# Four down-projection columns opened together at an FFN's end, and end columns that alternate between two pairs of PSUM banks

## The chip, the cores and the metric

The kernel runs on one core of a Trainium2 chip. The metric is the device time of one execution in microseconds (us), lower is better. The engines named below are TensorE (PE, matrix products; its weight loads are listed apart as PEld), VectorE (DVE), ScalarE (ACT), GpSimd (POOL) and SyncE (SP, which issues the transfers). SBUF is the core's working memory; PSUM is the accumulator memory that TensorE writes, eight banks of 128 partitions by 512 floats.

## The reference

A backbone of four layers (D = 1024) over 256 context tokens and 256 latent tokens. Each layer has a token mixer (0: windowed attention, 1: latent attention, 2: a gated linear recurrence, RG-LRU, 3: windowed attention again), and behind it a gated feed-forward network (FFN). Each of these eight stages ends in a projection back to 1024 columns whose gated result is added to the residual stream, and the next stage begins with an RMS norm of that stream.

```python
for layer in range(DEPTH):                      # DEPTH = 4
    kind, idx = layer % N_MIXERS, layer // N_MIXERS
    with_ctx_out = layer < DEPTH - 1
    ...
    h_lat = modulate(rmsnorm(x, norm1[layer]), sh1, sc1)
    h_ctx = modulate(rmsnorm(ctx, norm1[layer]), csh1, csc1)
    ...                                         # the mixer: y_lat, y_ctx (its last step is "... @ w_o")
    x = x + g1 * y_lat
    x = x + g2 * conv_ffn(modulate(rmsnorm(x, norm2[layer]), sh2, sc2), ...)
    if with_ctx_out:
        ctx = ctx + cg1 * y_ctx
        ctx = ctx + cg2 * conv_ffn(modulate(rmsnorm(ctx, norm2[layer]), csh2, csc2), ...)
return x

def conv_ffn(h, w_up, conv_w, conv_b, w_down):  # D_FF = 2816
    gate, val = jnp.split(h @ w_up, 2, axis=-1)
    gate = depthwise_conv(gate, conv_w, conv_b, FFN_CONV // 2)
    return (jax.nn.silu(gate) * val) @ w_down
```

The recurrent mixer projects h to a gate and an x branch (`lru_w_in`), convolves the x branch over four tokens, makes two sigmoid gates from it in each direction, scans, and projects the gated sum of both scans (`lru_w_out`).

## The kernel before

**Layout.** The residual stream is kept transposed, eight tiles `X[0..7]` of 128 columns by 512 tokens (0 to 255 context, 256 to 511 latent; layer 3 carries latents alone behind its mixer). A projection of all tokens is a product per 128 output columns, 512 wide.

**Products in three parts.** Each operand is kept as a high part (`hi`, rounded by ScalarE) and the rest (`lo`). `mm3` makes three TensorE products per pair of tiles: hi by hi (L227), the other side's lo (L228) and the weight's lo (L229). One output column of an FFN's last group with its four gated tiles is so 12 products.

**Weights.** SyncE loads a unit of 1024 columns (`raw`), ScalarE rounds it (`whi`, L214), GpSimd subtracts (`wlo`, L218). There are three buffers of `whi` and `wlo`: the unit after next can't be rounded before the products on the oldest one have run. A unit of the FFN's down projection (`fdn`) holds two output columns.

**PSUM.** Four pools with two banks each: `mm`, `fl`, `mo`, `tp`. A bank is free again when VectorE has added its column to X, at L452: `X = X + gate * column` ("x<-mo" in the profile, mo being the bank read).

**An FFN** goes through 22 gated tiles of 128 in groups, four in each but the first. ScalarE and VectorE make a gated tile (`fl`, L1117) and split it into `g_hi` (L261) and `g_lo` (L262). The products of a group with the down projection are made while the next group's up projections run; for the last group `out_tail` makes them.

**`out_tail`** ends every stage. It takes the eight output columns in units of `per` columns. In the layers that carry context the last three units' columns are made for the context half alone (256 wide) at first, and their weights are held; what is ahead of those is 512 wide. Then the next stage's norm is woven in: squares of the context half of X (ScalarE, L413) and their sum (VectorE, L415), two held columns for the latents (`lat(2)`), the sum over partitions (TensorE, L423), an inverse root of three Newton steps of VectorE on 128x2 numbers (L278, L268, L269, then L271 to L273 three times: `rs_v`, `rs_i`, `rs_y`, `rs_t`), its broadcast (TensorE, L427), the other held columns (`lat(99)`), and the normalised context (`hn`, L437). Attention stages end on `fl` banks (both ones), the FFNs and the recurrent layer on `mo` banks.

```python
for step, n in ((branch, 0), (branch, 1), (gates, 0), (branch, 2), (gates, 1), ...
lead = [(unit(("lix", m)), bank()) for m, bank in enumerate((fl_ps, fl_ps, mm_ps))]
```

**The recurrent layer** runs an order written by hand: `branch(n)` is the projection (`lix`, banks `fl`) and convolution (`xc`, L1001 and L1006) of two of eight column blocks, `gates(n)` the sigmoid gates (products of `x_hl` in banks `mm`, read at L1025) and the scans, `gate(n)` the GELU gate (`gg`, L1064). Its first three column blocks are made together ahead of it (`lead`). VectorE reads a block's bank four times (L1001, and L1006 for three taps) before it is free.

The order within each engine is set when the kernel is built: a scheduler puts the written order into one stream for each engine, and a free buffer of a pool is a condition of it.

Of the kernel before, what the change touches and what calls it, by code (L numbers as in the profile page):

```python
# [19 lines left out]
T = 512  # L20
NCTX = 256
DEPTH = 4
KT = D // 128
# [88 lines left out]
def hybrid_kernel(ctx: ExitStack, tc: tile.TileContext, xT, cc, ccT, W, modwa, modwb, modw, colv, rowv, tabs, band, out, depth=DEPTH, dbg=None):  # L112
# [43 lines left out]
    def mo_ps():  # L156
        return ps_mo.tile([128, T], F32, tag="mo", name="mo")

    def tp_ps():
        return ps_tp.tile([128, T], F32, tag="tp", name="tp")  # L160
# [3 lines left out]
    def dn_ps():  # L164
        turn[0] += 1
        return mo_ps() if turn[0] % 2 else tp_ps()

    X = [const.tile([128, T], F32, name=f"x{j}") for j in range(KT)]
    colt = const.tile([128, NCOLS], F32, name="colt")
# [274 lines left out]
                    nc.vector.scalar_tensor_tensor(lj, u, b, f32(hj), op0=ALU.add, op1=ALU.subtract)  # L444
            return op.ins

    def proj_cols(l, part, m, wt, src, sl, bank):
        ps = bank()
        mm3(ps[:, sl], [(wh, wl, sh[:, sl], sw[:, sl]) for (wh, wl), (sh, sw) in zip(wt, src)])
        for s, half in (CTX, LAT):  # L450
            if half.start >= sl.start and half.stop <= sl.stop:
                nc.vector.scalar_tensor_tensor(X[m][:, half], ps[:, half], modc[l][:, s, part + m:part + m + 1], X[m][:, half],  # L452
                                               op0=ALU.mult, op1=ALU.add)

    def out_tail(l, part, keys, per, src, t0, nxt, bank):
        n = len(src)

        def cols(z, wt):
            wh, wl = wt
            for m in range(z * per, (z + 1) * per):  # L460
                o = (m - z * per) * n
                yield m, [(wh[:, (o + k) * 128:(o + k + 1) * 128], wl[:, (o + k) * 128:(o + k + 1) * 128]) for k in range(n)]

        split_at = len(keys) if t0 else len(keys) - 3
        held = []
        for z, key in enumerate(keys):
            wt = unit(key)
            for m, w in cols(z, wt):
                proj_cols(l, part, m, w, src, slice(t0, T) if z < split_at else CTX[1], bank)
                if z >= split_at:  # L470
                    held.append((m, w))
        if held:
            todo = iter(held)

            def lat(k):
                for _ in range(k):
                    c = next(todo, None)
                    if c:
                        proj_cols(l, part, *c, src, LAT[1], bank)

            if isinstance(nxt, End):
                lat(99)
            else:
                nxt.tiles()
                sums = nxt.squares(1)
                lat(2)
                rb = nxt.rsq(sums)
                lat(99)
                nxt.apply(1, rb, range(KT))
                lat(99)  # L490
        nxt.half(0)
# [34 lines left out]
    def swa(l, i, q0, nm, nxt, first=None):  # L526
# [199 lines left out]
        for z, c in enumerate(cores[1]):  # L726
            core(*c)
            steps(mods, M1[z % len(M1)])
            for m in range(z * 8 // n, (z + 1) * 8 // n):
                half_proj(l, ("swo", i), m, units, tiles(*o[0]), q0 * 128)  # L730
        out_tail(l, 16, [("swo", i, 1, q) for q in range(4)], 2, tiles(*o[1]), q0 * 128, nxt, fl_ps)

    def mla(l, nm, nxt):
        hi, lo = nm.hi, nm.lo
# [194 lines left out]
        for hg in range(4):  # L929
            if hg < 3:  # L930
                group(hg + 1)
            for h in range(4):
# [9 lines left out]
                if hg == 3:  # L942
                    for m in (2 * h, 2 * h + 1):
                        half_proj(l, ("mwo",), m, units, tiles(*o[0]), 0)
        out_tail(l, 16, [("mwo", 1, q) for q in range(4)], 2, tiles(*o[1]), 0, nxt, fl_ps)

    def lru(l, nm, nxt):
        hi, lo = nm.hi, nm.lo
# [34 lines left out]
            in_part(wt, ps, slice(0, T))  # L983
            return ps

        lead = [(unit(("lix", m)), bank()) for m, bank in enumerate((fl_ps, fl_ps, mm_ps))]
        for _, sl in (CTX, LAT):
            for wt, ps in lead:
                in_part(wt, ps, sl)
# [77 lines left out]

        for step, n in ((branch, 0), (branch, 1), (gates, 0), (branch, 2), (gates, 1), (branch, 3), (gates, 2), (gate, 0), (gates, 3), (gate, 1), (merge, 0), (merge, 1), (gate, 2), (merge, 2), (gate, 3), (merge, 3)):
            step(n)
        out_tail(l, 16, [("lwo", m) for m in range(KT)], 1, tiles(rh[0], rl[0]) + tiles(rh[1], rl[1]), 0, nxt, mo_ps)  # L1070

    def ffn(l, t0, nm, nxt):
        hi, lo = nm.hi, nm.lo
# [72 lines left out]
                            next(mods, None)  # L1146
            pend = (a, b - a, gh, gl)
        a, n, gh, gl = pend
        out_tail(l, 40, [("fdn", l, a, q) for q in range(n)], KT // n, tiles(gh, gl, n), t0, nxt, mo_ps)

    def dump(n):
        if dbg is not None:
# [182 lines left out]
```

## Time and profile before

| | us |
|---|---|
| device time, median of three runs (2243.03 to 2250.57) | 2244.1 |
| profiled execution, its own time | 2239.54 |
| profiled execution, span of the trace | 2237.8 |
| TensorE busy in it | 2120.5 (95%) |
| VectorE busy | 1572.0 (70%) |
| ScalarE busy | 1033.3 (46%) |
| GpSimd busy | 1046.0 (47%) |

1.74 us of the profiled execution lie around its span. TensorE's records overlap by their pipelined ends, so that the busy share says where products run back to back, not how well; its idle time is what is to be read. In a row of the timeline the bracket gives the idle time of the engine ahead of that instruction and what ended it.

### The profile page before, as it was taken

The numbers are of one execution on the slowest core, as the hardware profiler recorded it, in microseconds if no ns is written. First come the engines' busy times: TensorE is split into PE (matmuls) and PEld (weight loads), VectorE is DVE, ScalarE is ACT, GpSimd is POOL, SyncE is SP. The second block draws the span as 40 slices with busy tenths as digits, with TensorE's granted clock in tenths as the row PEclk, the third lists the DMA queues.
The fourth block names the chain that finished last, engine by engine and source line by source line (L and its number), as shares of the span: only waits on it lengthen the run. The fifth ranks groups of instructions, "written<-read, shape, count | busy, mean of one in ns | idle before, by whom it ended". The sixth has DMA issues, their size and how long they took to land.

```text
span 2237.8 us, 32872 instructions
## 1 busy us (share of the span) xinstructions
PE 2120.5 (95%) x12084; PEld 1762.9 (79%) x12084; DVE 1572.0 (70%) x3342; ACT 1033.3 (46%) x1850; POOL 1046.0 (47%) x760
## 2 busy tenths in 40 slices
PE   6989999999999999999999998899999999898999
PEld 5666788888878666888888786688888887678999
DVE  4677779777776887687879689847864456785333
ACT  4467653332346775532323366634332234675544
POOL 3231155444544113444554456664544444526887
PEclk9999999999999999999999999999999999999999
DMA  8534136554532001155556422234655552313665
GB/s 300 195 123 133 39 131 193 170 173 164 174 101 68 21 29 57 60 194 175 175 179 189 140 67 81 78 93 136 194 185 167 164 168 74 104 38 107 187 181 158
DMA packets 83888, 300.14 MB, mean 134 GB/s; under 512 B 11152, under 2 KB 12816, under 8 KB 81296
## 3 DMA queue, kind: packets, MB, share of 16 engines
q1 hardware_dynamic: 83728, 298.05, 41.4%
q8 instruction: 95, 1.56, 0.3%
q14 instruction: 65, 0.53, 0.1%
HBM read 296.97 MB, written 1.05 MB: 133 GB/s over the span
## 4 chain that ended last, share of the span: by engine, by line
PE 76%; DVE 16%; ACT 4%; DMA 2%; issue 1%; POOL 1%; SPq 0%; ACTq 0%; DVEq 0%
PE fl L228 9%; PE fl L229 8%; PE fl L227 8%; PE mm L227 7%; PE mm L229 7%; PE mm L228 7%; PE mo L228 4%; PE mo L227 4%; PE mo L229 4%; PE tp L227 3%; PE tp L229 2%; PE tp L228 2%; PE mo L700 2%; PE mm L887 2%; PE tp L694 2%
## 5 line engine op out<-in xcount | busy, mean ns | idle before, releaser
L218 POOL TENSOR_TENSOR wlo<-raw,whi 128x256 fp32r<-128x256 f32 (+3 forms) x709 | 1011.4, 1448 | 1121.6 <-ACT whi L214 1086.0
L214 ACT ACTIVATE whi<-raw 128x1024 fp32r<-128x1024 f32 (+3 forms) x367 | 382.6, 1043 | 478.0 <-PE tp L228 187.8
L376 DVE SCALAR_TENSOR_TENSOR junk<-mw,cbc 128x1024 bf16<-128x1024 f32 x256 | 457.6, 1788 | 24.3 <-DMA mw<-in_modw_dram 14.7
L227 PE MATMUL fl<-h_hi,whi 128*128 128x512 f32 (+1 forms) x832 | 296.8, 358 | 3.3 <-DVE lam L961 1.7
L228 PE MATMUL fl<-h_lo,whi 128*128 128x512 f32 (+1 forms) x832 | 297.3, 358 | 0.2 <-POOL h_lo L442 0.2
L229 PE MATMUL fl<-h_hi,wlo 128*128 128x512 f32 (+1 forms) x832 | 297.2, 358 | 0.1
L228 PE MATMUL mm<-h_lo,whi 128*128 128x512 f32 (+1 forms) x768 | 269.8, 352 | 2.3 <-DVE h_lo L444 1.5
L227 PE MATMUL mm<-h_hi,whi 128*128 128x512 f32 (+1 forms) x768 | 270.6, 352 | 1.3 <-ACT h_hi L438 1.1
L229 PE MATMUL mm<-h_hi,wlo 128*128 128x512 f32 (+1 forms) x768 | 269.3, 351 | 0.0
L1112 DVE SCALAR_TENSOR_TENSOR conv<-mm,colt,conv 128x510 f32<-128x510 f32 (+1 forms) x88 | 59.8, 679 | 191.7 <-ACT conv L1110 191.7
L1116 ACT ACTIVATE conv<-conv 128x512 f32<-128x512 f32 (+1 forms) x88 | 51.0, 580 | 288.9 <-DVE conv L1114 288.9
L227 PEld LDWEIGHTS fl<-h_hi,whi 128*128 128x128 f32 x832 | 157.7, 190 | 26.2 <-DVE xc L1006 1.9
L228 PEld LDWEIGHTS fl<-h_lo,whi 128*128 128x128 f32 x832 | 158.2, 190 | 23.0 <-POOL h_lo L442 0.6
L229 PEld LDWEIGHTS fl<-h_hi,wlo 128*128 128x128 f32 x832 | 158.1, 190 | 22.9 <-POOL wlo L218 0.5
L227 PE MATMUL mo<-g_hi,whi 128*128 128x256 f32 (+1 forms) x488 | 164.8, 338 | 9.4 <-DVE x L452 6.3
L228 PE MATMUL mo<-g_lo,whi 128*128 128x256 f32 (+1 forms) x488 | 164.0, 336 | 0.4 <-DVE g_lo L262 0.4
L228 PEld LDWEIGHTS mm<-h_lo,whi 128*128 128x128 f32 x768 | 146.4, 191 | 22.8 <-DVE h_lo L444 2.3
L227 PEld LDWEIGHTS mm<-h_hi,whi 128*128 128x128 f32 x768 | 147.0, 191 | 21.0 <-ACT h_hi L438 1.9
L229 PE MATMUL mo<-g_hi,wlo 128*128 128x256 f32 (+1 forms) x488 | 163.5, 335 | 0.0
L229 PEld LDWEIGHTS mm<-h_hi,wlo 128*128 128x128 f32 x768 | 146.3, 191 | 18.6
L452 DVE SCALAR_TENSOR_TENSOR x<-mo,modc,x 128x256 f32<-128x256 f32 x212 | 95.4, 477 | 85.9 <-PE mo L229 85.6
L227 PEld LDWEIGHTS mo<-g_hi,whi 128*128 128x128 f32 x488 | 92.4, 190 | 21.9 <-DVE x L452 6.7
(313 smaller groups left out, 4376.0 us busy)
## 6 DMA issues: line engine op xcount, KB each, us to landing
raw<-in_W_dram SPq DMA_DIRECT2D x352, 512.0 KB, 3.6
mw<-in_modw_dram SPq DMA_DIRECT2D x144, 512.0 KB, 4.2
mw<-in_modwa_dram SPq DMA_DIRECT2D x8, 1024.0 KB, 16.2
mw<-in_modwb_dram SPq DMA_DIRECT2D x16, 512.0 KB, 4.7
mw<-in_modwb_dram SPq DMA_DIRECT2D x8, 1024.0 KB, 9.2
cbc<-in_cc_dram SPq DMA_DIRECT2D x3, 1024.0 KB, 5.8
raw<-in_W_dram SPq DMA_DIRECT2D x8, 384.0 KB, 3.0
x<-in_xT_dram SPq DMA_DIRECT2D x8, 256.0 KB, 3.7
```

Of the source, the lines that this page charges most:

```text
L214: nc.scalar.activation(hi, raw, AF.Copy)
L218: nc.gpsimd.tensor_tensor(lo[:, cs], raw[:, cs], f32(hi[:, cs]), op=ALU.subtract)
L227: nc.tensor.matmul(ps, ah, bh, start=start and i == 0, stop=False, **kw)
L228: nc.tensor.matmul(ps, ah, bl, start=False, stop=False, **kw)
L229: op = nc.tensor.matmul(ps, al, bh, start=False, stop=stop and i == n - 1, **kw)
L376: nc.vector.scalar_tensor_tensor(junk, raw, 1.0, cbc[:, s], op0=ALU.mult, op1=ALU.mult, accum_out=modc[l][:, s, m:m + 1])
L452: nc.vector.scalar_tensor_tensor(X[m][:, half], ps[:, half], modc[l][:, s, part + m:part + m + 1], X[m][:, half], op0=ALU.mult, op1=ALU.add)
L694: nc.tensor.transpose(pp[:, c:c + 128], P[z][:, (2 * kp + kk) * 128:(2 * kp + kk + 1) * 128], ident)
L700: nc.tensor.matmul(po[r], v[0][:, kb, p * 128 + 64 * z:p * 128 + 64 * z + 64], pt[:, kp, (kk * 2 + z) * 128:(kk * 2 + z + 1) * 128], start ...
L887: nc.tensor.matmul(ps[:, c], d["q"][:96, 2 * hp + z, bc], d["k"][:96, 2 * hp + z, :nk], start=True, stop=True)
L1112: op = nc.vector.scalar_tensor_tensor(y3[:, :, 1:], g3[:, :, :255], cw[:, l, 0, f:f + 1], y3[:, :, 1:], op0=ALU.mult, op1=ALU.add)
L1116: nc.scalar.activation(y[:, t0:], y[:, t0:], AF.Silu)
```

## The change

Four edits:

1. `tail_ps`, a new source of banks, alternates between `mo` and `fl`, four banks. The ends of the attention stages and of the recurrent layer take their columns from it.
2. An FFN's end takes columns 0 to 3 (two units of weights) in four banks at once (`opened`: mo, tp, mo, tp). All products with the first three gated tiles come first for these four columns, then the products with the last gated tile for each, then the additions to X. The other columns take `dn_ps` (mo and tp in turn), the held latent halves `tail_ps`.
3. `proj_cols` is split: its additions are `add_cols` now, which stands alone behind the opened columns.
4. The recurrent layer's three leading column blocks stand in banks mm, mm, fl, where they stood in fl, fl, mm.

```diff
+    def tail_ps():
+        turn[0] += 1
+        return mo_ps() if turn[0] % 2 else fl_ps()
...
-    def proj_cols(l, part, m, wt, src, sl, bank):
-        ps = bank()
-        mm3(ps[:, sl], [(wh, wl, sh[:, sl], sw[:, sl]) for (wh, wl), (sh, sw) in zip(wt, src)])
+    def add_cols(l, part, m, ps, sl):
         for s, half in (CTX, LAT):
             if half.start >= sl.start and half.stop <= sl.stop:
                 nc.vector.scalar_tensor_tensor(X[m][:, half], ps[:, half], modc[l][:, s, part + m:part + m + 1], X[m][:, half],
                                                op0=ALU.mult, op1=ALU.add)
...
-    def out_tail(l, part, keys, per, src, t0, nxt, bank):
+    def proj_cols(l, part, m, wt, src, sl, bank):
+        ps = bank()
+        mm3(ps[:, sl], [(wh, wl, sh[:, sl], sw[:, sl]) for (wh, wl), (sh, sw) in zip(wt, src)])
+        add_cols(l, part, m, ps, sl)
+
+    def out_tail(l, part, keys, per, src, t0, nxt, bank, last=None, opened=()):
         n = len(src)
...
-        for z, key in enumerate(keys):
-            wt = unit(key)
+
+        def begin(z):
+            wt = unit(keys[z])
+            got = []
             for m, w in cols(z, wt):
-                proj_cols(l, part, m, w, src, slice(t0, T) if z < split_at else CTX[1], bank)
+                sl = slice(t0, T) if z < split_at else CTX[1]
+                got.append((m, w, sl))
                 if z >= split_at:
                     held.append((m, w))
+            return got
+
+        z0 = 0
+        if opened:
+            z0 = len(opened) // per
+            parts = []
+            for z in range(z0):
+                for m, w, sl in begin(z):
+                    parts.append((m, w, sl, opened[m]()))
+
+            def term(w, k, sl):
+                return [(*w[k], src[k][0][:, sl], src[k][1][:, sl])]
+
+            for m, w, sl, ps in parts:
+                for k in range(n - 1):
+                    mm3(ps[:, sl], term(w, k, sl), start=k == 0, stop=False)
+            for m, w, sl, ps in parts:
+                mm3(ps[:, sl], term(w, n - 1, sl), start=False)
+                add_cols(l, part, m, ps, sl)
+        for z in range(z0, len(keys)):
+            for m, w, sl in begin(z):
+                proj_cols(l, part, m, w, src, sl, bank)
+        bank = last or bank
...
-        out_tail(l, 16, [("swo", i, 1, q) for q in range(4)], 2, tiles(*o[1]), q0 * 128, nxt, fl_ps)
+        out_tail(l, 16, [("swo", i, 1, q) for q in range(4)], 2, tiles(*o[1]), q0 * 128, nxt, tail_ps)
...
-        out_tail(l, 16, [("mwo", 1, q) for q in range(4)], 2, tiles(*o[1]), 0, nxt, fl_ps)
+        out_tail(l, 16, [("mwo", 1, q) for q in range(4)], 2, tiles(*o[1]), 0, nxt, tail_ps)
...
-        lead = [(unit(("lix", m)), bank()) for m, bank in enumerate((fl_ps, fl_ps, mm_ps))]
+        lead = [(unit(("lix", m)), bank()) for m, bank in enumerate((mm_ps, mm_ps, fl_ps))]
...
-        out_tail(l, 16, [("lwo", m) for m in range(KT)], 1, tiles(rh[0], rl[0]) + tiles(rh[1], rl[1]), 0, nxt, mo_ps)
+        out_tail(l, 16, [("lwo", m) for m in range(KT)], 1, tiles(rh[0], rl[0]) + tiles(rh[1], rl[1]), 0, nxt, tail_ps)
...
-        out_tail(l, 40, [("fdn", l, a, q) for q in range(n)], KT // n, tiles(gh, gl, n), t0, nxt, mo_ps)
+        out_tail(l, 40, [("fdn", l, a, q) for q in range(n)], KT // n, tiles(gh, gl, n), t0, nxt, dn_ps, tail_ps,
+                 (mo_ps, tp_ps, mo_ps, tp_ps))
```

What stands where, in the streams as built (the changed kernel's lines stand further down: its L231, L232, L233 are L227 to L229 of before, L454 is L452, L419 is L415).

TensorE at the end of layer 0's FFN, before: column 0 (bank `mo_5840`) makes its third and fourth gated tile's products and column 1 (`mo_5855`) begins; `g_hi_5375` and `g_lo_5376` hold all four gated tiles of the group.

```order
L227 MATMUL mo_5840<-g_hi_5375,whi_5836 128x512
L228 MATMUL mo_5840<-g_lo_5376,whi_5836 128x512
L229 MATMUL mo_5840<-g_hi_5375,wlo_5837 128x512
L227 MATMUL mo_5840<-g_hi_5375,whi_5836 128x512
L228 MATMUL mo_5840<-g_lo_5376,whi_5836 128x512
L229 MATMUL mo_5840<-g_hi_5375,wlo_5837 128x512
L227 MATMUL mo_5855<-g_hi_5375,whi_5836 128x512
L228 MATMUL mo_5855<-g_lo_5376,whi_5836 128x512
```

The same place now, from the last first-part product of column 3 (`tp_5849`) on: then the last gated tile's products of columns 0 to 3.

```order
L231 MATMUL tp_5849<-g_hi_5375,whi_5844 128x256
L232 MATMUL tp_5849<-g_lo_5376,whi_5844 128x256
L233 MATMUL tp_5849<-g_hi_5375,wlo_5845 128x256
L231 MATMUL mo_5840<-g_hi_5375,whi_5836 128x512
L232 MATMUL mo_5840<-g_lo_5376,whi_5836 128x512
L233 MATMUL mo_5840<-g_hi_5375,wlo_5837 128x512
L231 MATMUL tp_5841<-g_hi_5375,whi_5836 128x512
L232 MATMUL tp_5841<-g_lo_5376,whi_5836 128x512
L233 MATMUL tp_5841<-g_hi_5375,wlo_5837 128x512
L231 MATMUL mo_5848<-g_hi_5375,whi_5844 128x256
L232 MATMUL mo_5848<-g_lo_5376,whi_5844 128x256
L233 MATMUL mo_5848<-g_hi_5375,wlo_5845 128x256
```

The last gated tile's products of column 0 moved behind the 36 products that columns 0 to 3 make with the other three tiles; the number of products is the same.

VectorE at the same place, before: the two halves of columns 0 and 1 are added to X, then a sum of squares (`acc`) stands ahead of column 2.

```order
L262 TENSOR_TENSOR g_lo_5376<-fl_5801,g_hi_5375 128x512
L452 SCALAR_TENSOR_TENSOR x0_94<-mo_5840,modc0_124,x0_94 128x256 x2
L452 SCALAR_TENSOR_TENSOR x1_95<-mo_5855,modc0_124,x1_95 128x256 x2
L415 TENSOR_TENSOR acc_5976<-acc_5976,sq_5978 128x256
L452 SCALAR_TENSOR_TENSOR x2_96<-mo_5876,modc0_124,x2_96 128x256
L415 TENSOR_TENSOR P_6145<-P_6145,P_6147 128x256
L415 TENSOR_TENSOR acc_5976<-acc_5976,sq_5981 128x256
```

VectorE there now.

```order
L266 TENSOR_TENSOR g_lo_5376<-fl_5801,g_hi_5375 128x512
L454 SCALAR_TENSOR_TENSOR x0_94<-mo_5840,modc0_124,x0_94 128x256 x2
L454 SCALAR_TENSOR_TENSOR x1_95<-tp_5841,modc0_124,x1_95 128x256 x2
L454 SCALAR_TENSOR_TENSOR x2_96<-mo_5848,modc0_124,x2_96 128x256
L454 SCALAR_TENSOR_TENSOR x3_97<-tp_5849,modc0_124,x3_97 128x256
L419 TENSOR_TENSOR acc_5976<-acc_5976,sq_5978 128x256
L454 SCALAR_TENSOR_TENSOR x4_98<-mo_5910,modc0_124,x4_98 128x256
```

The additions of columns 2 and 3 moved ahead of the first sum of squares, and four banks are read where two were.

TensorE in the recurrent layer, around the third pair's gates, before: four products of the first GELU gate (`mo_12989`) stand between the gates' products (`mm_12902` and `mm_12927`, from `x_hl`).

```order
L229 MATMUL mm_12902<-x_hl_12581,wlo_12867 128x512
L227 MATMUL mo_12989<-h_hi_11942,whi_12982 128x512
L228 MATMUL mo_12989<-h_lo_11944,whi_12982 128x512
L229 MATMUL mo_12989<-h_hi_11942,wlo_12983 128x512
L227 MATMUL mo_12989<-h_hi_11942,whi_12982 128x512
L227 MATMUL mm_12927<-x_hl_12581,whi_12918 128x512
L228 MATMUL mm_12927<-x_hl_12581,whi_12918 128x512
```

There now: the last gate's products (`mm_12954`) run to their end, and the GELU gate begins behind them.

```order
L231 MATMUL mm_12954<-x_hl_12581,whi_12918 128x512
L232 MATMUL mm_12954<-x_hl_12581,whi_12918 128x512
L233 MATMUL mm_12954<-x_hl_12581,wlo_12919 128x512
L231 MATMUL mo_12989<-h_hi_11942,whi_12982 128x512
L232 MATMUL mo_12989<-h_lo_11944,whi_12982 128x512
L233 MATMUL mo_12989<-h_hi_11942,wlo_12983 128x512
```

The first GELU gate's first four products moved from within the third pair's gates to behind them. GpSimd's and SyncE's streams are the same as before.

## Rows read from the trace of the kernel before

**Rows 1.** The page: busy times, and the chain that ended last, by engine.

```profile
PE 2120.5 (95%) x12084; PEld 1762.9 (79%) x12084; DVE 1572.0 (70%) x3342; ACT 1033.3 (46%) x1850; POOL 1046.0 (47%) x760
...
PE 76%; DVE 16%; ACT 4%; DMA 2%; issue 1%; POOL 1%; SPq 0%; ACTq 0%; DVEq 0%
```

**Rows 2.** TensorE's waits: waited for, us in total, times, longest.

```profile
PE tp L427 <- DVE rs_y L273: 13.5, 11, 3.4
...
PE mo L227 <- ACT gg L1064: 8.8, 1, 8.8
...
PE mo L227 <- DVE x L452: 6.3, 8, 1.2
...
PE mo L227 <- ACT g_hi L261: 3.0, 2, 1.5
...
PE fl L227 <- DVE x L452: 2.1, 3, 0.9
```

**Rows 3.** Timeline of TensorE, end of layer 0's FFN: start, duration, [idle before].

```profile
633.97 0.50 PE L227 MATMUL mo<-g_hi,whi 128*128 128x512 f32 x1 [1.49 <-ACT g_hi L261]
634.69 0.50 PE L228 MATMUL mo<-g_lo,whi 128*128 128x512 f32 x1 [0.22 <-DVE g_lo L262]
...
642.29 0.38 PE L227 MATMUL mo<-g_hi,whi 128*128 128x256 f32 x1 [1.25 <-DVE x L452]
...
655.37 0.39 PE L227 MATMUL mo<-g_hi,whi 128*128 128x256 f32 x1 [0.42 <-DVE x L452]
...
657.58 0.71 PE L427 MATMUL tp<-tabt,rs_y 128*128 128x128 f32 x4 [0.98 <-DVE rs_y L273]
```

**Rows 4.** Windows of TensorE, three FFN ends: length, busy (products), PEclk, DMA, GB/s.

```profile
630.27:640.89 10.62, 8.91 (x49) 1.00 0.42 133
642.29:651.03 8.74, 8.74 (x73) 1.00 0.12 36
1855.54:1863.93 8.39, 8.39 (x48) 1.00 0.31 110
1865.50:1874.23 8.73, 8.73 (x72) 1.00 0.21 60
...
2222.48:2234.30 11.82, 11.72 (x97) 1.00 0.27 94
```

**Rows 5.** Timeline of VectorE, end of layer 0's FFN.

```profile
639.43 2.41 DVE L415 TENSOR_TENSOR acc<-acc,sq 128x256 f32<-128x256 f32 x1 [0.34 <-ACT sq L413]
...
644.02 0.43 DVE L415 TENSOR_TENSOR acc<-acc,sq 128x256 f32<-128x256 f32 x1 [0.48 <-ACT sq L413]
...
652.01 0.16 DVE L278 TENSOR_SCALAR rs_v<-tp 128x2 f32<-128x2 f32 x1 [0.30 <-PE tp L423]
...
656.88 0.64 DVE L273 SCALAR_TENSOR_TENSOR rs_y<-rs_t,rs_y 128x2 f32<-128x2 f32 x1
```

**Rows 6.** Timeline of ScalarE, end of layer 0's FFN.

```profile
633.34 0.58 ACT L261 ACTIVATE g_hi<-fl 128x512 fp32r<-128x512 f32 x1
638.04 1.06 ACT L214 ACTIVATE whi<-raw 128x1024 fp32r<-128x1024 f32 x1 [1.25 <-PE mo L228]
```

**Rows 7.** Timeline of GpSimd, end of layer 0's FFN.

```profile
639.17 2.39 POOL L218 TENSOR_TENSOR wlo<-raw,whi 128x1024 fp32r<-128x1024 f32 x1 [3.28 <-ACT whi L214]
```

**Rows 8.** Timeline of TensorE, end of layer 0's attention.

```profile
282.96 0.39 PE L227 MATMUL fl<-o,whi 128*128 128x256 f32 x1 [0.88 <-DVE x L452]
```

**Rows 9.** Timeline of VectorE at the same place.

```profile
279.14 0.16 DVE L278 TENSOR_SCALAR rs_v<-tp 128x2 f32<-128x2 f32 x1 [0.30 <-PE tp L423]
...
284.28 0.15 DVE L273 SCALAR_TENSOR_TENSOR rs_y<-rs_t,rs_y 128x2 f32<-128x2 f32 x1
```

**Rows 10.** Timeline of TensorE in the recurrent layer.

```profile
1321.80 0.47 PE L227 MATMUL fl<-h_hi,whi 128*128 128x512 f32 x1 [1.73 <-DVE lam L961]
...
1383.58 0.80 PE L227 MATMUL mm<-x_hl,whi 128*128 128x512 f32 x1 [6.19 <-ACT ex L1025]
```

**Rows 11.** A window of VectorE in the recurrent layer: length, busy (instructions).

```profile
1316.00:1350.00 34.00, 30.89 (x43) 1.00 0.31 93
```

## What the change should do to the time: the prediction

> **What bounds the kernel now.** The page comes first: TensorE is busy 95% of the span, and the chain that ended last lies on it for 76%, on VectorE for 16% [rows 1]. The change adds and removes no product, so that it can only take TensorE's idle time, some 5%, or move it. Where that time lies is in TensorE's waits: 6.3 us for additions to X that free an mo bank, 3.0 us for the last gated tile, 2.1 us for fl banks, 13.5 us for the inverse root, 8.8 us once for a GELU [rows 2]. The change aims at the first three. What each is worth depends on what ends last behind it, which the timelines of the stage ends tell.
>
> At the end of layer 0's FFN TensorE stops at three places in the columns [rows 3]: 1.49 us in column 0 for `g_hi`, 0.22 us for `g_lo`, and 1.25 us ahead of column 4, whose mo bank VectorE hasn't read. The last is a chain of three engines. The fourth weight unit is rounded at 638.04, when the oldest buffer is released [rows 6]; GpSimd subtracts for 2.39 us from 639.17 [rows 7]; VectorE's sum of squares beside it takes 2.41 us where its like takes 0.43 us [rows 5], and the addition that TensorE waits for stands behind that sum. So the four columns take 10.62 us with 8.91 us of work, and the next 72 products, up to the sum over partitions (L423), start 1.40 us behind their end [rows 4].
>
> **The change part by part, FFN ends.** The FFN of layer 2 shows the four columns without the gated tile's wait: 8.39 us for 24 products of 512 and 24 of 256 columns, and 72 products of 256 take 8.73 us [rows 4]. That is 0.121 us a short product and (8.39 - 24 x 0.121) / 24 = 0.228 us a long one.
>
> - *Last gated tile.* Now 18 long and 18 short products stand ahead of it: 18 x 0.228 + 18 x 0.121 = 6.3 us. The stage begins at 630.27, so it is asked for at 636.6. `g_hi` is there at 633.34 + 0.58 = 633.92 [rows 6], and the product with `g_lo` could start at 634.69 [rows 3]. The wait is gone with some 2 us to spare.
> - *Bank wait.* Column 4 takes the bank of column 0. Column 0's last product is over at about 636.6 + 3 x 0.228 + 0.2 = 637.5, and two additions, each about as long as the undisturbed sum of the same size, 0.43 us [rows 5], free the bank by 638.4; TensorE comes to it at 630.27 + 8.39 = 638.66. Columns 5, 6 and 7 have banks of which the additions stand ahead of the first sum of squares now. The sum will still be blocked beside GpSimd, but the addition behind it (column 4's) is needed for a bank only much later. The wait is gone.
> - *Weights.* Buffer 0 is now released by the last product of column 1, at 638.66 - 6 x 0.121 = 637.9, where rounding began at 638.04 before. So the fourth unit's low part is ready at about 637.9 + 1.06 + 2.39 = 641.4; column 6 needs it at 638.66 + 24 x 0.121 + 0.24 = 641.8. It just holds, by 0.4 us.
>
> The Trainium skill (SBUF — State Buffer, Who interferes with whom) says that a VectorE instruction with two inputs in SBUF is blocked by a GpSimd instruction that reads SBUF, and one with a single SBUF input isn't. The 2.41 us sum agrees. By that rule the four additions that now stand ahead of the sum, with one input in PSUM, run through GpSimd's subtraction.
>
> The sum over partitions then starts at 630.27 + 8.39 + 8.73 = 647.4 where it started at 651.03: 3.6 us. Behind it VectorE goes from 652.01 to 657.52 through the inverse root without a pause [rows 5]. The 0.42 us ahead of a held column at 655.37 may go through the other banks, but the broadcast waits for the root all the same, and its 0.98 us [rows 3] becomes so much longer. So nothing is won behind the sum: **-3.6 us**.
>
> Layer 1's FFN waits the same way: `g_hi` is waited for in 2 places, 3.0 us in total, longest 1.5, and the longest waits for mo banks are 1.2 [rows 2]; its timeline reads alike. **-3.6 us**. Layer 2's has no gated tile's wait: from 1855.54 to 1874.23 it takes 18.69 us [rows 4], and without the bank wait 8.39 + 8.73 = 17.12: **-1.6 us**. Layer 3's makes 96 products in 11.82 us with 11.72 busy [rows 4]: nothing to take, **0**; four opened columns add nothing either, as the same products run.
>
> **Attention ends.** They wait 0.88 us for an fl bank once [rows 8], in layers 0 and 1, but between the sum over partitions and the end of the root, 279.14 to 284.43, VectorE has work all along [rows 9], and the broadcast waits for that. With more banks the products end sooner and the broadcast starts as before: **0** for both. In layer 3 (2.1 - 2 x 0.88 = 0.34 us) I put **-0.2**, half of it.
>
> The Trainium skill (Perfetto Trace Analysis, Matmuls) says that independent groups of products should rotate through different banks, so that reading out one overlaps the next. By that rule alone every wait for an addition to X would go, at the attention ends too; the rows on the root say no. It is rival B.
>
> **Recurrent layer.** Its end has no bank wait worth naming, so `tail_ps` is worth 0 there. The lead's banks are another matter. The fourth column block waits 1.73 us for an fl bank that VectorE reads [rows 10], and with the lead in mm, mm, fl a free fl bank is there. But VectorE is busy 30.89 of 34 us in that stretch [rows 11], so TensorE's gain is mostly lost again behind it. In exchange the gates' mm banks come free only when two blocks are read out. And four products that filled a pause of the gates now stand behind them. I bound the sum by one whole wait won, -1.7, and by two such waits lost, +3.5; since VectorE paces the stretch I take a third of the wait won, **-0.5**.
>
> **Sum:** -3.6 - 3.6 - 1.6 - 0.2 - 0.5 = -9.5 us. Against the profiled 2239.54 that is 2230.0; the median of the runs shown is 2244.1, 4.6 above the profiled one, which gives **2235**. 0.3% is 6.7 us, about what a measurement of this kernel can tell from no change.
>
> **Rivals.**
>
> - *B: every bank wait goes.* 0.88 twice, the rest of the mo waits (6.3 - 3 x 1.25 = 2.55), and 1.2 more at the recurrent lead on top of the forecast: -9.5 - 1.8 - 2.55 - 1.2 = -15, **2229**. For it: four banks at each end. Against it: the root's chain on VectorE [rows 5, 9].
> - *C: the recurrent layer gives it back.* Its gates wait up to 6.19 us for ScalarE's reading of mm banks [rows 10], and 8.8 us for the GELU's [rows 2]; the change alters the order of just these. One more wait of the first kind makes -9.5 + 6.2 = -3.3, **2241**: no change that can be told.
> - *D: the ends give half back.* The weights' spare 0.4 us is small. If the rounding comes late because squares stand ahead of it on ScalarE, or VectorE's additions fall behind, a new wait of 1.25 to 1.5 us comes in each of three FFN ends, **2239 to 2240**.
> - *E: slower.* The recurrent layer's gates are a loop over ScalarE, VectorE and TensorE. If taking mm banks for the lead makes each of the four gates steps wait as at 1383.58, it costs 3 x 6.19 = 18.6 us more; from 16.2 us on it is over 0.3% slower: -9.5 + 18.6 = +9, **2253**. Against it: VectorE's pace leaves TensorE slack there, and the lead is used once.
>
> **How the numbers follow.** Forecast 0.55 (its own range 2231 to 2238), B 0.10, C 0.22, D 0.08, E 0.05. The range from 2228 takes in B; up to 2243 it takes in D and C, whose own price could be a little above one wait. E and larger mishaps stay out, with a part of C. Faster by over 0.3% is below 2237.4: B and nearly all of the forecast's case, 0.62. Within 0.3%: C, D and the rest, 0.32. Slower: E, 0.06.
>
> **What would show it.** In the changed profile the waits for `g_hi` and `g_lo` at FFN ends are gone, and each such end takes 17.1 us from its first product to L423's place in layers 0, 1 and 2. The three 1.25 us waits for x are gone; that for the root grows by about 0.4 us in each FFN end. If the attention ends are shorter by 0.88 us, B is right. If column 6 waits for `wlo`, it is D. If the sum of waits for `ex`, `xc` or `gg` in the recurrent layer grows by more than 3 us, it is C, and by more than 16, E. The prediction is wrong above all if the recurrent layer, which I could only bound, moves by more than its bounds.

## The result, and the profile after

The changed kernel takes 2227.47 us (median of 4 runs, 2226.69 to 2228.39), the kernel before beside it 2243.57 us (4 runs, 2242.37 to 2250.57). The ratio is 0.9931, 95% interval 0.9912 to 0.9951: 11.0 to 19.7 us saved, where 9.5 were forecast. 2235 was said, and the median lies half a microsecond below the range's lower end of 2228; 0.9931 of the 2244.1 us from which the range was laid is 2228.6. The two profiled executions differ less, 2239.54 and 2228.39, by 11.2 us; the trace's span is 2226.6 us now.

The page after, busy times and the chain by engine, against [rows 1]: VectorE's share of the chain fell from 16% to 12%.

```profile
PE 2113.2 (95%) x12084; PEld 1760.3 (79%) x12084; DVE 1563.7 (70%) x3342; ACT 1032.2 (46%) x1850; POOL 1044.8 (47%) x760
...
PE 78%; DVE 12%; ACT 3%; DMA 3%; issue 2%; POOL 2%; SPq 0%; ACTq 0%; DVEq 0%; POOLq 0%
```

TensorE's waits after (us in total, times, longest), against [rows 2].

```profile
PE tp L431 <- DVE rs_y L277: 18.8, 11, 3.8
...
PE mo L231 <- ACT gg L1097: 5.7, 1, 5.7
PE mm L231 <- ACT ex L1058: 5.7, 1, 5.7
PE fl L233 <- POOL wlo L222: 4.9, 2, 2.5
...
PE tp L231 <- DVE x L454: 1.5, 2, 0.8
...
PE mo L231 <- DVE x L454: 0.6, 1, 0.6
```

The waits for `g_hi` are gone, those of mo banks for an addition to X fell from 6.3 to 0.6 us and those of fl banks are gone; two at tp banks, 1.5 us, stood at 0.8 us before. The waits for the root rose from 13.5 to 18.8 us in the same 11 places: what was taken ahead of the root came back there in part. New are 4.9 us for a weight's low part at fl banks and 1.2 us at a mo bank, in the recurrent layer.

The FFN ends of layers 0, 1 and 2, from the first product to the sum over partitions: windows of TensorE, with length, busy (products), PEclk, DMA share, GB/s.

```profile
631.12:648.09 16.97, 16.97 (x121) 1.00 0.32 101
1265.29:1282.26 16.97, 16.97 (x122) 1.00 0.40 125
1848.67:1865.64 16.97, 16.97 (x121) 1.00 0.28 83
```

All three are 16.97 us with TensorE busy throughout. Before they were 20.75 (630.27 to 651.03, [rows 4]), 20.73 and 18.69: 3.78 + 3.76 + 1.72 = 9.3 us saved in three places, in every execution alike (below).

VectorE, then TensorE and GpSimd, at the end of layer 0's FFN, against [rows 3, 5, 7].

```profile
639.83 0.47 DVE L454 SCALAR_TENSOR_TENSOR x<-mo,modc,x 128x256 f32<-128x256 f32 x1
640.22 0.47 DVE L454 SCALAR_TENSOR_TENSOR x<-tp,modc,x 128x256 f32<-128x256 f32 x1
640.61 1.98 DVE L419 TENSOR_TENSOR acc<-acc,sq 128x256 f32<-128x256 f32 x1
...
649.28 0.78 DVE L272 TENSOR_SCALAR rs_i<-rs_v 128x2 int32<-128x2 int32 x1
650.09 0.73 DVE L273 TENSOR_SCALAR rs_y<-rs_i 128x2 int32<-128x2 int32 x1
...
652.49 0.16 DVE L275 TENSOR_TENSOR rs_t<-rs_y 128x2 f32<-128x2 f32 x1
```

```profile
654.64 0.71 PE L431 MATMUL tp<-tabt,rs_y 128*128 128x128 f32 x4 [1.67 <-DVE rs_y L277]
```

```profile
639.90 2.42 POOL L222 TENSOR_TENSOR wlo<-raw,whi 128x1024 fp32r<-128x1024 f32 x1 [3.15 <-ACT whi L218]
...
649.22 2.35 POOL L222 TENSOR_TENSOR wlo<-raw,whi 128x288 fp32r<-128x288 f32 x3 [6.91 <-ACT whi L218]
```

Two additions (639.83, 640.22) run at 0.47 us each beside GpSimd's subtraction that starts at 639.90; the sum behind them is stretched to 1.98 us by it, and nobody waits for that now. From the sum over partitions to the broadcast it is 654.64 - 648.09 = 6.55 us, as before (657.58 - 651.03 = 6.55): nothing was won there, and the wait for the root grew from 0.98 to 1.67 us.

### The profile page after: what moved, and what is told of

The parts are those of the page before. It is cut to its first block, busy times and chain, and to the rows that moved or that the text cites. A ratio compares the mean times of both kernels' runs of the same rounds, so it can differ in the third digit from the quotient of the medians.

```text
span 2226.6 us, 32884 instructions
## 1 busy us (share of the span) xinstructions
PE 2113.2 (95%) x12084; PEld 1760.3 (79%) x12084; DVE 1563.7 (70%) x3342; ACT 1032.2 (46%) x1850; POOL 1044.8 (47%) x760
## 4 chain that ended last, share of the span: by engine, by line
PE 78%; DVE 12%; ACT 3%; DMA 3%; issue 2%; POOL 2%; SPq 0%; ACTq 0%; DVEq 0%; POOLq 0%
PE fl L232 9%; PE fl L233 9%; PE fl L231 9%; PE mm L233 7%; PE mm L232 7%; PE mm L231 7%; PE mo L231 4%; PE mo L232 4%; PE mo L233 4%; PE tp L231 3%; PE tp L232 3%; PE tp L233 3%; PE mo L733 2%; POOL wlo L222 2%; PE mm L920 2%
## 5 line engine op out<-in xcount | busy, mean ns | idle before, releaser
L222 POOL TENSOR_TENSOR wlo<-raw,whi 128x256 fp32r<-128x256 f32 (+3 forms) x709 | 1010.1, 1446 | 1113.3 <-ACT whi L218 1075.1
L233 PE MATMUL fl<-h_hi,wlo 128*128 128x512 f32 (+1 forms) x816 | 293.4, 360 | 4.9 <-POOL wlo L222 4.9
L231 PE MATMUL fl<-h_hi,whi 128*128 128x512 f32 (+1 forms) x816 | 293.2, 359 | 1.5 <-DVE xc L1039 1.3
L232 PE MATMUL fl<-h_lo,whi 128*128 128x512 f32 (+1 forms) x816 | 293.2, 359 | 0.0
L232 PE MATMUL mm<-h_lo,whi 128*128 128x512 f32 (+1 forms) x784 | 274.1, 351 | 2.5 <-DVE h_lo L448 1.5
L231 PE MATMUL mm<-h_hi,whi 128*128 128x512 f32 (+1 forms) x784 | 273.9, 351 | 1.2 <-ACT h_hi L442 1.1
L233 PE MATMUL mm<-h_hi,wlo 128*128 128x512 f32 (+1 forms) x784 | 273.5, 349 | 0.0
L233 PEld LDWEIGHTS fl<-h_hi,wlo 128*128 128x128 f32 x816 | 155.0, 190 | 28.6 <-POOL wlo L222 6.1
L231 PEld LDWEIGHTS fl<-h_hi,whi 128*128 128x128 f32 x816 | 155.3, 190 | 24.3 <-ACT P L1058 1.7
L232 PEld LDWEIGHTS fl<-h_lo,whi 128*128 128x128 f32 x816 | 155.0, 190 | 22.1
L232 PEld LDWEIGHTS mm<-h_lo,whi 128*128 128x128 f32 x784 | 149.4, 191 | 23.5 <-POOL h_lo L446 2.5
L231 PEld LDWEIGHTS mm<-h_hi,whi 128*128 128x128 f32 x784 | 149.4, 191 | 20.8 <-ACT h_hi L442 2.1
L233 PEld LDWEIGHTS mm<-h_hi,wlo 128*128 128x128 f32 x784 | 149.5, 191 | 18.6
L454 DVE SCALAR_TENSOR_TENSOR x<-mo,modc,x 128x256 f32<-128x256 f32 x197 | 88.3, 476 | 87.4 <-PE mo L233 87.1
L231 PE MATMUL mo<-g_hi,whi 128*128 128x512 f32 (+1 forms) x388 | 134.3, 346 | 0.6 <-DVE x L454 0.6
L232 PE MATMUL mo<-g_lo,whi 128*128 128x512 f32 (+1 forms) x388 | 134.4, 346 | 0.0
L233 PE MATMUL mo<-g_hi,wlo 128*128 128x512 f32 (+1 forms) x388 | 134.3, 346 | 0.0
L231 PE MATMUL tp<-g_hi,whi 128*128 128x512 f32 (+1 forms) x352 | 124.0, 352 | 1.5 <-DVE x L454 1.5
```

The costliest lines, as they stand in the source:

```text
L222: nc.gpsimd.tensor_tensor(lo[:, cs], raw[:, cs], f32(hi[:, cs]), op=ALU.subtract)
L231: nc.tensor.matmul(ps, ah, bh, start=start and i == 0, stop=False, **kw)
L232: nc.tensor.matmul(ps, ah, bl, start=False, stop=False, **kw)
L233: op = nc.tensor.matmul(ps, al, bh, start=False, stop=stop and i == n - 1, **kw)
```

## The experiments

Each was run beside the kernel before on the same chip, and "saved" is against that. The first four, in one series:

**The changed kernel once more** (no edit).

> The changed kernel once more, in five rounds beside the kernel before. Theory P (the profiled pair tells the whole change): 10 to 12 us faster, as its two profiles (2239.54 and 2228.39) differ by 11.2; the 16 us between the two medians is then spread of the executions. Theory Q (more is won than the pair of profiles shows): 15 to 17 us faster again, and the profiled execution of before was a lucky one.

Measured: 2226.16 us against 2240.16, ratio 0.9938 (0.9923 to 0.9954), 10.3 to 17.2 us saved. Neither theory is excluded: the interval holds P's 10 to 12 and Q's 15 to 17.

**The FFN ends alone.** The other three calls and the lead are put back:

```diff
-        out_tail(l, 16, [("swo", i, 1, q) for q in range(4)], 2, tiles(*o[1]), q0 * 128, nxt, tail_ps)
+        out_tail(l, 16, [("swo", i, 1, q) for q in range(4)], 2, tiles(*o[1]), q0 * 128, nxt, fl_ps)
...
-        lead = [(unit(("lix", m)), bank()) for m, bank in enumerate((mm_ps, mm_ps, fl_ps))]
+        lead = [(unit(("lix", m)), bank()) for m, bank in enumerate((fl_ps, fl_ps, mm_ps))]
```

> Only the FFN ends are changed (four opened columns, last gated tile last, held latent halves on mo and fl); attention ends, the recurrent layer's end and its lead stand as before. Theory P: the FFN ends of layers 0, 1 and 2 give 3.7 + 3.4 + 1.5 us, 8.6 us faster, within 7 to 10. Rival R (recurrent layer's new banks carry the gain): under 5 us.

Measured: 2220.36 us, ratio 0.9914 (0.9898 to 0.9931), 15.5 to 22.8 us saved. R falls: the gain doesn't come from the recurrent layer's new banks. But it is more than P's 7 to 10, and by the medians (19.8 us) more than the 14.0 us of the whole change in the same series; the two intervals overlap. The next series asks why.

**The attention ends and the recurrent layer's end alone** on mo and fl; the FFN call and the lead as before:

```diff
-        out_tail(l, 40, [("fdn", l, a, q) for q in range(n)], KT // n, tiles(gh, gl, n), t0, nxt, dn_ps, tail_ps,
-                 (mo_ps, tp_ps, mo_ps, tp_ps))
+        out_tail(l, 40, [("fdn", l, a, q) for q in range(n)], KT // n, tiles(gh, gl, n), t0, nxt, mo_ps)
```

> Only the ends of the attention stages and of the recurrent layer take mo and fl in turn; FFN ends and lead as before. Theory P (the inverse root on VectorE paces these ends): within 1 us of the kernel before, the waits of 0.88 us for x gone in the profile and the waits for the root longer by the same. Rival B (bank waits set the ends): 1.8 to 2.1 us faster.

Measured: 2239.69 us, ratio 0.9998 (0.9987 to 1.0009). In this kernel's timeline of TensorE the broadcast at layer 0's attention end waits for the root 1.58 us, where it waited 0.43 us before (the first line): the wait for x ([rows 8], 0.88 us) is gone, and the time up to the broadcast is the same.

```profile
284.48 0.71 PE L427 MATMUL tp<-tabt,rs_y 128*128 128x128 f32 x4 [0.43 <-DVE rs_y L273]
```

```profile
283.46 0.71 PE L431 MATMUL tp<-tabt,rs_y 128*128 128x128 f32 x4 [1.58 <-DVE rs_y L277]
```

From the sum to the broadcast it is 6.34 us (277.12 to 283.46) as before (278.15 to 284.48, 6.33). At layer 1's attention end it is 6.33 and 6.34 us. The times alone, from 2.9 us saved to 2.0 lost, would leave room for B's 1.8 to 2.1; the timeline leaves none. P holds, and the rule of rotating banks (B) gives nothing where the root ends last.

**The recurrent layer's lead alone** in mm, mm, fl.

> Only the recurrent layer's first three column blocks stand in mm, mm, fl; all ends as before. Theory P: 0 to 2 us faster (the profiled pair gives 0.95 us for this layer), the 1.73 us wait for an fl bank gone and partly given back at the gates. Rival R: 4 us faster or more. Rival C: slower by up to 3.5 us.

Measured: 2238.86 us, ratio 0.9988 (0.9976 to 1.0): 0 to 5.4 us saved. P's 0 to 2 and R's 4 us lie in the interval, C does not.

The second series takes the FFN ends apart, and adds the other parts to them one by one.

**FFN ends and lead**, the ends of the other stages as before.

> The FFN ends' edit and the recurrent layer's lead in mm, mm, fl; attention ends on fl, the recurrent layer's end on mo as before. Theory S (the parts add up, and what differs beyond that is spread of the executions): the profiled stages give 8.6 + 1 to 3, so 9 to 14 us faster than before and the same as the whole change. Rival I (the lead takes back 6 us once the FFN ends are open): 13 to 15 us faster where the FFN ends alone give 20.

Measured: 2227.81 us against 2240.99, ratio 0.994 (0.9925 to 0.9955), 10.1 to 16.8 us saved. That holds most of S's 9 to 14 and all of I's 13 to 15.

**FFN ends and the other stages' ends**, the lead as before.

> The FFN ends' edit and the banks in turn at the attention ends and the recurrent layer's end; lead as before. Theory S: 8 to 13 us faster, as with the FFN ends alone. Rival J (the banks in turn cost 6 us once the FFN ends are open): 13 to 15 us where the FFN ends alone give 20.

Measured: 2225.05 us, ratio 0.993 (0.9916 to 0.9945), 12.3 to 18.8 us saved: above most of S's 8 to 13, and J's 13 to 15 lies in it.

**Four banks, but no postponing:** the last gated tile's products stand in their column again.

```diff
             for m, w, sl, ps in parts:
-                for k in range(n - 1):
-                    mm3(ps[:, sl], term(w, k, sl), start=k == 0, stop=False)
-            for m, w, sl, ps in parts:
-                mm3(ps[:, sl], term(w, n - 1, sl), start=False)
+                for k in range(n):
+                    mm3(ps[:, sl], term(w, k, sl), start=k == 0, stop=k == n - 1)
                 add_cols(l, part, m, ps, sl)
```

> FFN ends alone, four banks, but each column's products in one go, so the last gated tile is met in column 0 as before. By the prediction's terms only the bank waits of 1.25 us with their restart go, 1.4 us in three FFN ends: 4.2 us faster, and the waits for the last gated tile stay at 1.5 and 0.2 us in two places. Rival (postponing is not needed, a free bank lets column 1 go ahead): 8 us faster or more.

Measured: 2230.91 us, ratio 0.996 (0.9946 to 0.9974), 5.8 to 12.1 us saved. Its windows of the three FFN ends:

```profile
628.65:647.93 19.28, 17.56 (x122) 1.00 0.27 89
1266.27:1285.51 19.24, 17.53 (x122) 1.00 0.32 110
1846.81:1864.01 17.20, 17.20 (x121) 1.00 0.24 82
```

20.75 - 19.28 = 1.5, 20.73 - 19.24 = 1.5 and 18.69 - 17.20 = 1.5 us: the bank term is as sized (1.4), 4.5 us in the three ends. The waits for `g_hi` stay (3.0 us in two places), so that the rival's column 1 did not go ahead. The whole gain is larger than 4.5, so something outside the ends moved too.

**Postponing over two columns only,** in two mo banks (`dn_ps, tail_ps, (mo, tp, mo, tp)` of the FFN call becomes `mo_ps, None, (mo_ps, mo_ps)`).

> FFN ends alone, the last gated tile's products last, but over columns 0 and 1 only and in two mo banks; the other columns as before. By the prediction's terms the waits for the last gated tile go but for 0.1 to 0.3 us (18 long products cover 4.1 us), 2 us in each of two FFN ends, less some 0.4 us ahead of column 2, whose bank is read late now, in three; the 1.25 us waits stay: 2.5 to 4 us faster. Rival (four columns are needed for cover): under 1.5 us.

Measured: 2237.0 us, ratio 0.9978 (0.9968 to 0.9988), 2.7 to 7.2 us saved. Its windows:

```profile
636.45:655.15 18.70, 17.68 (x121) 1.00 0.29 92
1273.79:1292.50 18.71, 17.68 (x121) 1.00 0.34 113
1858.13:1876.61 18.48, 17.45 (x122) 1.00 0.25 76
```

2.05, 2.02 and 0.2 us: the last gated tile's wait is worth 2 us with its restart, bank waits apart, and two columns cover it; the time lies as expected, above the rival's 1.5. With the banks that is 3.5 us of the 3.8 that four columns give.

**The recurrent layer in eleven executions.** The traces show what moved outside the ends in the kernel with four banks and no postponing: in the kernels whose FFN ends take four banks (held halves on mo and fl), the scheduler orders VectorE, ScalarE and TensorE anew within the recurrent layer, whose code is untouched. Which of these banks does it no run separates; with two mo banks (two columns) the order is as before. With the lead in mm, mm, fl the layer has a third order. So the profiles fall into three groups. Windows from the latents' broadcast ahead of the layer to the context's broadcast at its end, for before, the changed kernel, and FFN ends with other stages' ends (one fence each):

```profile
1308.21:1511.18 202.97, 179.40 (x874) 0.96 0.27 81
```

```profile
1302.02:1504.04 202.02, 179.29 (x873) 0.97 0.27 81
```

```profile
1302.89:1501.44 198.55, 179.44 (x876) 0.96 0.27 83
```

| order of the recurrent layer | its length in each profile, us | mean | mean with the stretch ahead |
|---|---|---|---|
| as before (before, other ends alone, two columns) | 202.97, 202.80, 202.86 | 202.9 | 214.5 |
| moved by the FFN ends, lead as before (FFN ends alone twice, with other ends, no postponing) | 200.01, 198.56, 198.55, 198.52 | 198.9 | 210.9 |
| lead in mm, mm, fl (lead alone, changed kernel twice, FFN ends and lead) | 199.20, 202.02, 200.60, 203.07 | 201.2 | 214.2 |

The second group saves 4.0 us that no line of the diff is meant for. It makes the kernel without postponing add up: 4.5 + 4.0 = 8.5, measured 5.8 to 12.1. The third group, to which the change as a whole belongs, saves 1.7 on average and spreads over 3.9 us.

These windows leave out the stretch ahead, from the context's broadcast to the latents', in which the lead's first products stand. Before, and after:

```profile
1296.62:1308.21 11.59, 10.87 (x82) 1.00 0.39 121
```

```profile
1288.88:1302.02 13.14, 12.42 (x83) 0.87 0.32 107
```

It is 11.6 us at a granted clock of 1.00 in six of the eleven profiles, and 12.6 to 13.1 us at 0.86 to 0.87 in the other five, all four with the new lead and the one of FFN ends with the other stages' ends: part of it runs at the lower of the clock's two levels (1.2 GHz) there. Ahead of it TensorE waited 1.1 to 1.9 us for the root, but as long in kernels where the clock stayed, so what decides it isn't shown. With this stretch the third group saves 0.3 us on average. What it pays with in the layer is seen in the waits: 6.5 us for `wlo` (L222) in the lead alone and 4.9 in the changed kernel, 0.2 in the FFN ends with other ends, while the wait for `gg` falls from 8.8 to 2.8 and 5.7 with it. That the lead takes 2 to 3 us back once the FFN ends are open is so suggested by the profiles; the times alone (12.3 to 18.8 us without, 10.1 to 16.8 with it) don't tell the two apart.

**The FFN ends alone, again,** in a third series.

> The FFN ends alone once more (the same kernel as the run named e1_ffn_only). Theory S (spread): 12 to 16 us faster than before, as the whole change, with the FFN ends in the profile as short as in it. Rival I/J (the other parts take 4 to 6 us back): 19 to 20 us faster again.

Measured: 2225.8 us against 2242.61, ratio 0.9928 (0.9912 to 0.9944), 12.6 to 19.7 us saved. The median is 16.8 us where it was 19.8 in the first series, and the interval holds S's 12 to 16 from 12.6 on and I/J's 19 to 20 in part: neither is excluded.

**The inverse root in PSUM,** to test that the root paces the ends. Each instruction now has at most one operand in SBUF:

```diff
+    def root_in_psum(ps):
+        v, i, t = (ps[:, 16 * z:16 * z + 2] for z in range(1, 4))
+        y = small(2, "rs_y")
+        nc.vector.tensor_scalar(v, ps[:, 0:2], 1.0 / D, EPS, op0=ALU.mult, op1=ALU.add)
...
+            nc.vector.tensor_tensor(t, v, y, op=ALU.mult)
+            nc.vector.scalar_tensor_tensor(t, t, -0.5, y, op0=ALU.mult, op1=ALU.mult)
+            nc.vector.scalar_tensor_tensor(y, t, 1.5, y, op0=ALU.add, op1=ALU.mult)
...
-            rs = mean_rsqrt(ps[:, 0:2], 2, D)
+            rs = root_in_psum(ps)
```

> The whole change, and the numbers of the norms' inverse root (128x2) in spare columns of the PSUM bank that holds the sums, so that each of its VectorE instructions reads at most one operand from SBUF; the number of instructions stays. Theory V (the root paces the stage ends, and what stretches it are GpSimd's subtractions beside it, 0.64 to 0.78 us an instruction where 0.16 us is usual): the instructions stay at 0.2 us, the waits for the root fall from 18.8 us in 11 places to under 9, and the kernel is 8 to 12 us faster than the whole change alone. Rival W (the root is long for its own sake, twelve dependent instructions with others between): under 2 us.

Measured: 2213.25 us against 2242.61, ratio 0.9877 (0.9864 to 0.9891), 24.4 to 30.5 us faster than before. At layer 0's FFN end the timelines of VectorE, GpSimd and TensorE; then, for the whole kernel, the group of one line (45 instructions, ns min/median/max) and TensorE's waits for the root:

```profile
646.33 0.17 DVE L289 TENSOR_SCALAR tp<-tp 128x2 int32<-128x2 int32 x1
646.53 0.16 DVE L290 TENSOR_SCALAR rs_y<-tp 128x2 int32<-128x2 int32 x1
646.61 0.75 DVE L431 TENSOR_TENSOR P<-P 128x256 f32<-128x256 f32 x1
```

```profile
646.27 2.52 POOL L222 TENSOR_TENSOR wlo<-raw,whi 128x288 fp32r<-128x288 f32 x3 [6.91 <-ACT whi L218]
```

```profile
651.25 0.71 PE L443 MATMUL tp<-tabt,rs_y 128*128 128x128 f32 x4 [0.27 <-DVE rs_y L294]
```

```profile
L292 DVE TENSOR_TENSOR tp<-tp,rs_y x45: 152/168/169, 15.1 to 2013.3; 128x2 f32<-128x2 f32 x45
```

```profile
PE tp L443 <- DVE rs_y L294: 5.6, 4, 2.5
```

Beside the same subtraction of GpSimd the root's instructions take 0.16 to 0.17 us where 0.73 and 0.78 stood; none of the 45 is over 0.169. The sum with both operands in SBUF is still stretched, to 0.75. The waits for the root fall from 18.8 to 5.6 us; in part they come back as waits for an addition to X at mo banks, 4.5 us where 0.6 stood. V's mechanism holds, and W is excluded; against the whole change it is some 13 to 15 us by the medians, more than V's 8 to 12.

The profiles tell where most of it lies. From the sum to the context's broadcast all seven stage ends are shorter than in the changed kernel: this FFN end by 0.4 us (6.11), the attention ends of layers 0 and 1 and layer 2's FFN end by 1.0 each (5.32), layer 1's FFN end by 1.3, the recurrent layer's by 2.5, layer 3's attention end by 0.8, 8 us together. The stretch from there to the latents' broadcast is 1.6 to 1.7 us shorter behind the attention stages of layers 0 and 1 and layer 2's FFN, 2.5 ahead of the recurrent layer (1.5 of it the clock, which is at 1.00 here), and within 0.3 us at the other two. The built order moved in the recurrent layer as well (197.5 us, 2.5 of the difference to 202.0 at its end), so that the 13 us are not the root's alone.

**The root in PSUM in the kernel before,** the same edit.

> The kernel before with the inverse root alone in PSUM. Theory V: the waits for the root were 13.5 us here and fall to under 7; but with two banks at the attention ends the 0.88 us waits for x stay, so less than in the changed kernel is won: 4 to 8 us faster. Rival W: under 2 us.

Measured: 2220.53 us, ratio 0.9908 (0.9893 to 0.9923), 17.3 to 24.0 us saved, waits for the root 5.6 us. More than V's 4 to 8: the same two stretches of every stage end are 14 us shorter together, of which V counted waits alone. The order of the streams changed here too (the recurrent layer is 197.2 us, 2.5 of the 5.7 us at its end), so the size is open; the direction isn't.

**FFN ends alone with the root in PSUM,** both edits as above.

> The FFN ends' edit with the inverse root in PSUM; attention ends on fl, the recurrent layer's end on mo and its lead as before. Theory K (with a short root the two fl banks of the attention ends come to bind, so that the banks in turn are worth something now): 2 to 4 us slower than the whole change with the root in PSUM (27 us faster than before), so 23 to 25 us faster than before, with waits for x at fl banks of 0.8 us and more in the profile. Rival L (the banks in turn and the lead are worth nothing with either root): 26 to 29 us faster than before.

Measured: 2217.47 us against 2238.9, ratio 0.9893 (0.9875 to 0.9912), 19.7 to 28.0 us faster than before. K's 23 to 25 lies in it, L's 26 to 29 in part; the waits for x at fl banks are 0.6 us in total, in two places, not the 0.8 us each that K named. Whether the other parts of the change are worth anything with a short root stays open. The kernel with the whole change and the root in PSUM has the lowest median of all, 2213.25 us, beside another series of the kernel before.

## Why the prediction came out as it did

**Last gated tile, bank wait, weights: right.** 17.12 us were worked out for an FFN end, 16.97 came, in all six executions with the edit alone or with other parts. The terms were -3.6, -3.6, -1.6 (8.8) and measured 3.8, 3.8, 1.7 (9.3). The parts were right one by one: 1.4 said and 1.5 measured for the bank, some 2 said and 2.0 measured for the last tile. The fourth unit's low part is ready at 639.90 + 2.42 = 642.32 and first needed at 642.57, 0.25 us to spare where 0.4 was said, and no product waited: D did not happen. (D's own terms give 2238 to 2239, not the 2239 to 2240 that was said.)

**Nothing won behind the sum: right.** 6.55 us before and after. The root's wait grew by 0.7 us at layer 0 rather than 0.4: the 0.42 us ahead of a held column went into it, and 0.3 us more.

**Attention ends at 0: right,** shown by the timeline of the kernel with them alone (6.34 us from the sum to the broadcast, 6.33 before), which its ratio of 0.9998 fits. B's mechanism was refuted there: banks that rotate give nothing where the next step waits for the root. The -0.2 for layer 3 is too small for these runs.

**Last FFN, 0: right;** from layer 3's last broadcast to the end it is 199.0 us before (2038.74 to the span's end) and 198.5 after.

**The recurrent layer, -0.5 within -1.7 to +3.5: near in size, by another path.** The 1.73 us wait of [rows 10] is gone. From the latents' broadcast on, the pair of profiles shows -0.95 and the four with this lead -1.7 on average, down to -3.7 for the lead alone. With the stretch ahead, where the lead's first products stand, the pair shows +0.6 and the four -0.3 on average, from -2.2 to +1.7. That this lies near -0.5 is luck. The step that failed is "since VectorE paces the stretch I take a third of the wait won": the layer's length moved with the order of its streams, where waits for `ex` (7.6 us before, the line below) and `gg` (8.8) shrank to 5.7 us each and waits for `wlo` came, and ahead of it the clock took 1.0 to 1.5 us back, a term that the prediction didn't have. The sign that was named for C and E, more waiting for `ex`, `xc` or `gg`, did not come.

```profile
PE mm L227 <- ACT ex L1025: 7.6, 4, 6.2
```

**The total: short by 4.5 to 6.6 us.** 9.3 + 0.3 = 9.6 is what the stages that the change aims at account for, almost what was forecast; the two series with the changed kernel give 11.0 to 19.7 and 10.3 to 17.2, by their medians 16.1 and 14.0. In the profiled pair, 11.2 us apart, 9.3 lie at the FFN ends and 2.1 in layer 3's attention stage, the recurrent layer takes 0.6 back, and the other stages move by up to 1.5 us either way, 0.4 us faster together. What the prediction left out are stretches at the lower level of the clock, which fall elsewhere in each execution. Layer 3's attention stage, whose order is the same up to its end, is 145.25 us in the profile before and 143.17 in the one after, at a granted clock of 0.95 and 0.97:

```profile
1893.49:2038.74 145.25, 127.28 (x862) 0.95 0.24 71
```

```profile
1884.91:2028.08 143.17, 124.62 (x863) 0.97 0.24 71
```

With the FFN ends alone it was 146.17 us at 0.93 once and 143.25 at 0.97 the other time, in the same kernel. Over the eleven profiles it is 143.0 to 143.3 us in six of the seven whose FFN ends take four banks, and 144.3 to 146.3 in the four others, so that this part may go with the change; but the kernel before with the root in PSUM has 142.1, and no run shows a way. Layer 0's attention stage, ahead of the first FFN end, differs as well, 259.4 to 267.5 us from the first broadcast to the sum at its end. And in the four profiles with the FFN ends of before (one of them with the root in PSUM), two of twelve such ends took 22.3 us at a granted clock of 0.92; it fell right after the 1.5 us wait for `g_hi`. The 24 ends with postponing over four columns, in eight profiles, are all 16.97 us. Whether the change makes stretches at the lower level rarer on average, and how much of the remaining 4.4 to 6.5 us that would be, the runs don't show.

## What to carry to other kernels

Price a wait with what ends last behind it: the same 0.9 to 1.5 us bank wait was worth all of itself at FFN ends, where it stood ahead of the sum over partitions, and nothing at attention ends, where it stood behind the sum, beside a chain of twelve small VectorE instructions that ended later. Postponing the one late operand over all columns that have banks is cheap, and for that operand two columns were enough. Where a scheduler sets the order, an edit at one stage's end can reorder the next stage whose code is untouched; compare the built streams there before the trace's difference is put down to the edit.

## What the hardware showed unexpectedly

The root's instructions on 128x2 numbers took 0.64 to 0.78 us beside GpSimd's subtraction when their operands lay in SBUF, and 0.14 to 0.17 us beside the same subtraction with all but one in PSUM. The Trainium skill (SBUF — State Buffer, Who interferes with whom) has the rule that a VectorE instruction with a single SBUF input outside its 2-port modes does not contend with GpSimd; these 45 instructions of a line, none over 0.169 us, agree. Two of the stretched ones, `rs_i` and `rs_y` (0.78 and 0.73 us), have a single SBUF input as well; by the rule they would have run in a 2-port mode, which no run here shows. In the kernel before the root in PSUM saved 17.3 to 24.0 us, where the whole change saved 10.3 to 17.2 and 11.0 to 19.7; how much of that is the root's own and how much the order that it moved stays open.
